# Gathering the next group inside the current one, taps behind the first projection weights, and the 64-row way back first

## Chip, core and metric

The kernel runs on one core of a Trainium2 chip. The core has five engines that matter here: PE (TensorE, matrix products), DVE (VectorE), ACT (ScalarE), POOL (GpSimd) and SP (SyncE, which here only issues DMAs). Data comes from HBM by 16 DMA engines. The metric is the time of one execution on the device, in microseconds.

## What is computed

Two layers over 256 tokens of width 1024, all in float32. The even layer mixes by a gated DeltaNet and a 2-D DFT, the odd layer by a Conformer convolution; both end in the same mixture of experts. Cut to what matters:

```
for l in range(2):
    h = rmsnorm(x) * (1 + sc1) + sh1
    mix = hybrid_mixer(h, ...) if l == 0 else conformer_conv(h, w1, b1, dw_w, ..., w2, b2)
    x = x + g1 * mix
    x = x + g2 * moe_ffn(rmsnorm(x) * (1 + sc2) + sh2, ...)

def conformer_conv(h, w1, ...):            # w1 is 1024 x 2048, dw_w has 31 taps per channel
    val, gate = split(h @ w1 + b1)
    u = depthwise_conv(val * sigmoid(gate), dw_w) + dw_b
    return silu(layernorm(u)) @ w2 + b2

def moe_ffn(t, ...):                       # 32 experts in 8 groups of 4; a token takes 2 experts of one group
    for e in range(32):
        hid = silu(t @ w_gate[e]) * (t @ w_up[e])       # 1024 -> 512
        y = y + combine[:, e] * (hid @ w_down[e])       # 512 -> 1024
```

The weights of the 64 experts are 384 MB, nearly all that is read.

## The kernel before

**The weight ring.** All large weights pass through one ring of 17 slots of 1 MB (tiles `rb`, `rx`, `ra`, `rc`). The list `plan` holds the units in the order of their transfers; an expert is six units (gate and up in two halves each, then down in two). `Ring.pump` (L232) issues the next unit as soon as a slot is free, all on SP's queue, and `Ring.done` frees slots after their last reader. A unit of kind "z" takes a slot without a transfer, as room for a result.

**A layer's experts.** `moe(l)` goes through the 8 groups. How many tokens chose group g is known only on the chip, so for each group the code holds five programs (`ARMS`): for up to 32 tokens, 64, 64 and 32 side by side, 128, and 128 twice. `arms` picks one by compare-and-branch on every engine; each program ends with a jump out over the others. In the profiled execution group 4 of layer 0 and groups 4 and 5 of layer 1 run the 64+32 program, groups 0 and 6 of layer 0 the 64-row one, and the other eleven the 32-row one.

**The gather.** `place` (L1276) brings a group's tokens together: DVE makes a one-hot `oh`, sixteen products with it fill two PSUM banks `px` (L1286), ACT and DVE copy these to `xg`, and a few small products give the combine weights and the transposed one-hot `oc`. `prep(g + 1)` stands behind group g's program, before the jump into the next one. `xg` and `oc` are double, by the parity of the group.

**A group's program** (`group`). For each of its four experts: gate and up products in two halves (`gate_up`, L1345 for 32 rows and L1347 for 64), `hidden` (SiLU on ACT, then a product with the combine weight on DVE), and between the halves of the next expert the down products of the last one (`down`): transposes `pth`, a copy `hT` on DVE, the products `yacc` (L1375 for 32 rows, L1385 for 64). A 64+32 group has two parts, which share the weights. At the end `close` copies `yacc` to `ysb`, and `scatter` is the way back: for each of eight blocks `pso` of the output, one product for each part (L1431) and one DVE operation that adds it to the stream `xT` (L1432).

**Into the odd layer.** In the last group of layer 0 the way back also writes the convolution's input `z`. The projection w1 (`conf_w`) is four blocks of two units; the first two blocks (four units) serve the first half of the channels. The convolution goes by transforms of the taps: `taps_transform`, which needs the taps (two transfers of 31 rows of 4 KB) and the table `dft` (1 MB), stands in PE's program right behind the first tile of the projection (L1540), before the second tile.

Of the kernel before, what the change touches and what calls it, by code (L numbers as in the profile page):

```python
# [310 lines left out]
def build(nc, tc, A, ctx, dbg=None):  # L311
# [39 lines left out]
    ident = C("ident")  # L351
# [138 lines left out]
    with ExitStack() as c0:  # L490
# [29 lines left out]
        add("x", [lambda t: [(t[32 * q:32 * q + 31, 0:1024], A["taps"]) for q in range(2)], A["dft"]])  # L520
        add("w", blk(A["conf_w1"], 0) + blk(A["conf_w1"], 2))
        add("z", [None] * 2)
        add("w", blk(A["conf_w1"], 1) + blk(A["conf_w1"], 3))
# [648 lines left out]
    def moe(l):  # L1172
        with ExitStack() as c1:
# [126 lines left out]
            class Part:  # L1300
# [61 lines left out]
                def down(self, us, hid, j):  # L1362
                    n, first, last = self.n, j == 0, j == 3
                    pt = pg.tile([P, 512], F32, name="pth", tag="tr")
                    hT = m2.tile([P, 4, 128], F32, name="hT", tag="hT")
                    if n == 32:
                        for i in range(2):
                            te.transpose(pt[:, 64 * i:64 * i + 64], hid[:, 128 * i:128 * i + 128], ident[0:64, 0:64])  # L1368
                        hT = hT[:, 0]
                        ve.tensor_copy(hT, pt[:, 0:128])  # L1370
# [6 lines left out]
                    for k in range(4):  # L1377
                        te.transpose(pt[:, n * k:n * k + n], hid[:, 128 * k:128 * k + 128], ident[0:n, 0:n])
                    ve.tensor_copy(hT[:, :, 0:n], pt[:, 0:4 * n].rearrange("p (k s) -> p k s", k=4))
# [37 lines left out]
            def scatter(parts, sums):  # L1417
# [4 lines left out]
                if sums and l == 0:  # L1422
                    zid, zt = ring.take(2, "z")
                    for h, t in enumerate(zt):
                        ve.tensor_copy(t[:, 0:1028].rearrange("p (k c) -> p k c", c=257)[:, :, 256:257], MOD(1, 0)[:, 4 * h:4 * h + 4].unsqueeze(2))
                    zs.append((zid, [t[:, 257 * i:257 * i + 257] for t in zt for i in range(4)]))
                for i, k in enumerate(KORD):
                    o = ps[k // 2][:, 256 * (k % 2):256 * (k % 2) + 256]
                    for p_ in parts:
                        a, b = p_.back(k)  # L1430
                        te.matmul(o, a, b, start=p_ is parts[0], stop=p_ is parts[-1])  # L1431
# [15 lines left out]
            def group(g, arm):  # L1447
# [11 lines left out]
                def tail(j, ids, us, hids):  # L1459
                    for p_, hid in zip(parts, hids):  # L1460
                        p_.down(us, hid, j)
                    ring.done(ids[4:])

                late = None
                for j in range(4):
# [5 lines left out]
                    if late:  # L1471
                        tail(*late)
                    for p_ in parts:
# [29 lines left out]
            for g in range(8):  # L1503
# [4 lines left out]
                if g < 7:  # L1508
                    prep(g + 1)
# [274 lines left out]
```

## Time and profile before

| | |
|---|---|
| median of 3 runs | 1555.91 us (1552.68 to 1557.39) |
| profiled execution | 1556.92 us, of it 1555.0 us span |
| PE busy | 1260.5 us (81%) |
| DVE, ACT, POOL busy | 478.0, 239.6, 152.5 us |
| DMA | 489.68 MB, mean 315 GB/s over the span |

The span is the time from the first to the last instruction in the trace, and all times of the trace are counted from its start. The experts of layer 0 take about 360 to 860 us, the convolution up to 1020 us, the experts of layer 1 the rest. Busy shares are means over stages with different limits; the rows further down are by stage.

### The profile page before, as it was taken

Reading aid. Unit: us, or ns where it says so; the run is one execution under the profiler, and the core shown is the slowest. Engines: PE = TensorE matmul, PEld = TensorE weight load, DVE = VectorE, ACT = ScalarE, POOL = GpSimd, SP = SyncE. Lnnn points to the kernel's source line nnn. Section 1 sums busy time; section 2 is a strip of 40 time slices with the busy share of each in tenths; the row PEclk is TensorE's granted clock in tenths of the full one; section 3 lists DMA queues with packets and bytes.
Section 4 is the critical chain, followed back from the end, with each engine's and each line's share of the span. In section 5 each row is a group of like instructions: output and inputs, shape, how many; then the busy total and the mean of one; then the engine's idle time right before and its main releaser. Section 6 shows DMA issues by size and latency. Waiting matters only on the chain.

```text
span 1555.0 us, 25396 instructions
## 1 busy us (share of the span) xinstructions
PE 1260.5 (81%) x10776; PEld 731.9 (47%) x10776; DVE 478.0 (31%) x1340; ACT 239.6 (15%) x530; POOL 152.5 (10%) x124
## 2 busy tenths in 40 slices
PE   6886999987986666998777499797667679899974
PEld 2443666665554333345444377664344233433542
DVE  3479898773111101012011312321101011201112
ACT  3333333213000000001001201320000000000101
POOL 0556553100000000000000100100000000000000
PEclk8889899987987777999899699998777789899876
DMA  9556665458999999997999942249999999579695
GB/s 351 188 197 215 210 218 187 149 203 336 416 410 415 414 415 413 408 364 299 413 415 406 332 176 108 109 181 414 415 414 414 415 413 409 233 298 352 251 412 207
DMA packets 109446, 489.68 MB, mean 315 GB/s; under 512 B 9474, under 2 KB 19970, under 8 KB 75968
## 3 DMA queue, kind: packets, MB, share of 16 engines
q1 hardware_dynamic: 109248, 487.08, 80.1%
q8 instruction: 120, 1.97, 0.5%
q14 instruction: 78, 0.64, 0.1%
HBM read 486.00 MB, written 1.05 MB: 313 GB/s over the span
## 4 chain that ended last, share of the span: by engine, by line
PE 55%; DMA 29%; DVE 9%; issue 3%; POOL 2%; ACT 2%; SPq 0%; DVEq 0%; ACTq 0%; POOLq 0%
PE gu L1347 10%; PE gu L1345 8%; DMA rb<-down 5%; PE yacc L1385 5%; DMA ra<-up 4%; DMA rc<-up 4%; PE yacc L1375 3%; PE pu L1666 3%; DMA rb<-gate 3%; PE pso L1431 3%; DMA rx<-up 2%; PE pu L1706 2%; PE pp L1040 2%; DMA rb<-up 1%; DMA rc<-down 1%
## 5 line engine op out<-in xcount | busy, mean ns | idle before, releaser
L1345 PE MATMUL gu<-rb,xg 128*32 128x256 f32 x1840 | 159.0, 416 | 33.8 <-DMA rb<-gate 9.9
L1358 DVE SCALAR_TENSOR_TENSOR hid<-sg,dup,gu 64x256 f32<-64x256 f32 (+1 forms) x76 | 42.0, 552 | 444.0 <-ACT sg L1357 357.0
L1357 ACT ACTIVATE sg<-gu 64x256 f32<-64x256 f32 (+1 forms) x76 | 32.9, 433 | 563.1 <-PE gu L1345 343.4
L1347 PE MATMUL gu<-rb,xg 128*64 128x512 f32 x368 | 110.0, 630 | 11.8 <-DMA rc<-gate 4.8
L1345 PEld LDWEIGHTS gu<-rb,xg 128*32 128x32 f32 x1840 | 72.3, 117 | 94.7 <-issue 43.1
L604 POOL TENSOR_TENSOR rc<-rc,sbc 128x1024 f32<-128x1024 f32 x36 | 89.6, 2494 | 42.4 <-DMA rc<-ada_t 42.2
L1345 PE MATMUL gu<-rx,xg 128*32 128x256 f32 x624 | 75.0, 420 | 13.5 <-DMA rx<-gate 4.6
L1040 PE MATMUL pp<-h,ra 128*128 128x512 f32 (+1 forms) x192 | 79.8, 557 | 4.9 <-DVE vtm L1026 4.9
L1431 PE MATMUL pso<-dup,ysb 32*128 32x256 f32 (+1 forms) x304 | 69.5, 463 | 14.2 <-ACT ysb L1401 6.3
L1345 PE MATMUL gu<-ra,xg 128*32 128x256 f32 x656 | 66.8, 430 | 17.0 <-DMA ra<-gate 9.2
L1432 DVE SCALAR_TENSOR_TENSOR xT<-pso,mods,xT 128x256 f32<-128x256 f32 x128 | 53.4, 478 | 64.8 <-PE pso L1431 64.7
L607 DVE SCALAR_TENSOR_TENSOR rc<-rc,sbc 128x1024 f32<-128x1024 f32 x44 | 65.5, 1492 | 4.0 <-DMA rc<-ada_t 3.9
L1345 PE MATMUL gu<-rc,xg 128*32 128x256 f32 x464 | 54.8, 449 | 13.0 <-DMA rc<-gate 8.9
L1375 PE MATMUL yacc<-rb,hT 128*32 128x256 f32 x976 | 61.9, 387 | 2.7 <-DVE hT L1370 2.7
L1347 PEld LDWEIGHTS gu<-rb,xg 128*64 128x64 f32 x368 | 35.4, 143 | 56.9 <-issue 50.5
L1431 PEld LDWEIGHTS pso<-dup,ysb 32*128 32x128 f32 (+1 forms) x304 | 34.7, 196 | 47.7 <-issue 14.6
L1370 DVE COPY hT<-pth 128x128 f32<-128x128 f32 x56 | 16.3, 290 | 131.7 <-PE pth L1368 131.7
L1040 PEld LDWEIGHTS pp<-h,ra 128*128 128x128 f32 x192 | 36.9, 201 | 39.3 <-issue 31.7
L415 POOL TENSOR_TENSOR ttok<-ttok 128x256 f32<-128x256 f32 x4 | 3.0, 752 | 528.8 <-ACT ttok L413 528.7
L1442 POOL TENSOR_TENSOR rb<-xT,a 128x256 f32<-128x256 f32 x5 | 3.4, 691 | 499.3 <-DMA rb<-conf_w 498.9
L1345 PEld LDWEIGHTS gu<-rx,xg 128*32 128x32 f32 x624 | 31.9, 118 | 36.1 <-issue 14.4
L1345 PEld LDWEIGHTS gu<-ra,xg 128*32 128x32 f32 x656 | 28.9, 120 | 41.1 <-issue 13.4
(719 smaller groups left out, 1955.6 us busy)
## 6 DMA issues: line engine op xcount, KB each, us to landing
rb<-down SPq DMA_DIRECT2D x70, 1024.0 KB, 20.1
rb<-gate SPq DMA_DIRECT2D x67, 1024.0 KB, 20.0
rb<-up SPq DMA_DIRECT2D x65, 1024.0 KB, 20.0
rc<-ada_t SPq DMA_DIRECT2D x80, 512.0 KB, 4.4
ra<-gate SPq DMA_DIRECT2D x24, 1024.0 KB, 18.3
ra<-up SPq DMA_DIRECT2D x24, 1024.0 KB, 17.0
rx<-down SPq DMA_DIRECT2D x24, 1024.0 KB, 15.4
rx<-up SPq DMA_DIRECT2D x23, 1024.0 KB, 20.0
```

The source lines that it names most:

```text
L604: ge.tensor_tensor(w, w, sbc, op=ALU.mult)
L607: ve.scalar_tensor_tensor(w, w, 1.0, sbc, op0=ALU.mult, op1=ALU.mult, accum_out=mods[:, l, j:j + 1])
L1040: te.matmul(pp[:, 0:n], w[:, k, o:o + 128], h[:, k, 512 - n:512], start=k == 0, stop=k == KT - 1)
L1345: te.matmul(self.out[o:o + 32], x, w[:, 256 * fh:256 * fh + 256], **how)
L1347: te.matmul(self.out[hf], x, w, **how)
L1357: se.activation(sg, g, AF.Silu)
L1358: ve.scalar_tensor_tensor(hid, sg, self.cw[:, j:j + 1], u, op0=ALU.mult, op1=ALU.mult)
L1375: te.matmul(self.y[32 * q:32 * q + 32], hT[:, o:o + 32], w[:, 256 * q:256 * q + 256], start=first and k == 0, stop=last and k == 3)
L1385: te.matmul(y[hf], hT[:, k, 0:n], w[:, 512 * hf:512 * hf + 512], start=(alone or first) and k == 0, stop=(alone or last) and k == 3)
L1431: te.matmul(o, a, b, start=p_ is parts[0], stop=p_ is parts[-1])
L1432: ve.scalar_tensor_tensor(xT[:, k, :], o, g2[:, k:k + 1], xT[:, k, :], op0=ALU.mult, op1=ALU.add)
L1666: te.matmul(pvg[hf], (wv, wg)[hf](k, 128 * i, 128 * i + 128), h1[:, k], start=k == 0, stop=k == KT - 1)
```

## The change

Three things. The gather of the next group moves from behind the group's program into it: into the third expert, between the down products of the second and the second half of the gate and up products. In the plan, the taps and dft move behind the first four projection units and the two z units. In a group with several parts, all parts are now transposed first (`turn`) before the down products, and on the way back all eight products of the first part come before those of the last.

```
@@ plan
-        add("x", [lambda t: [(t[32 * q:32 * q + 31, 0:1024], A["taps"]) for q in range(2)], A["dft"]])
         add("w", blk(A["conf_w1"], 0) + blk(A["conf_w1"], 2))
         add("z", [None] * 2)
+        add("x", [lambda t: [(t[32 * q:32 * q + 31, 0:1024], A["taps"]) for q in range(2)], A["dft"]])
         add("w", blk(A["conf_w1"], 1) + blk(A["conf_w1"], 3))
@@ Part
-                def down(self, us, hid, j):
+                def turn(self, hid):
...
+                    return hT
+
+                def down(self, us, hT, j):
...
@@ scatter
+                O = lambda k: ps[k // 2][:, 256 * (k % 2):256 * (k % 2) + 256]
+
+                for p_ in parts[:-1]:
+                    for k in KORD:
+                        te.matmul(O(k), *p_.back(k), start=p_ is parts[0] and k % 2 == 0, stop=False, skip_group_check=True)
                 for i, k in enumerate(KORD):
-                    o = ps[k // 2][:, 256 * (k % 2):256 * (k % 2) + 256]
-                    for p_ in parts:
-                        a, b = p_.back(k)
-                        te.matmul(o, a, b, start=p_ is parts[0], stop=p_ is parts[-1])
+                    o = O(k)
+                    te.matmul(o, *parts[-1].back(k), start=len(parts) == 1, stop=True, skip_group_check=len(parts) > 1)
@@ group
                 def tail(j, ids, us, hids):
-                    for p_, hid in zip(parts, hids):
-                        p_.down(us, hid, j)
+                    turned = [p_.turn(hid) for p_, hid in zip(parts, hids)]
+                    for p_, hT in zip(parts, turned):
+                        p_.down(us, hT, j)
...
                     if late:
                         tail(*late)
+                    if j == 2 and g < 7:
+                        prep(g + 1)
                     for p_ in parts:
                         p_.gate_up(us, 1)
@@ moe
                 arms(g, regs[g], 0, len(ARMS))
-                if g < 7:
-                    prep(g + 1)
```

How instructions move on two engines, first at the one place of SP's queue. This is SP's program in the 32-row program of layer 0's last group, before (`down` are the last expert's units, numbers are the slots):

```order
L250 DMA ra_127<-down 128x2x1024
L250 DMA ra_126<-down 128x2x1024
L246 DMA rx_2661<-taps 31x1024 x2
L250 DMA rb_3023<-dft 128x2048
L250 DMA rb_3024<-conf_w 128x4x512
L250 DMA rb_3025<-conf_w 128x4x512
L250 DMA rb_3026<-conf_w 128x4x512
L250 DMA rb_3027<-conf_w 128x4x512
L250 DMA rb_3030<-conf_w 128x4x512
```

and in the changed kernel:

```order
L250 DMA ra_127<-down 128x2x1024
L250 DMA ra_126<-down 128x2x1024
L250 DMA rx_2661<-conf_w 128x4x512
L250 DMA rb_3023<-conf_w 128x4x512
L250 DMA rb_3024<-conf_w 128x4x512
L250 DMA rb_3025<-conf_w 128x4x512
L246 DMA rb_3028<-taps 31x1024 x2
L250 DMA rb_3029<-dft 128x2048
L250 DMA rb_3030<-conf_w 128x4x512
```

Four units of the projection are now ahead of the taps and dft, and nothing else is in another place. On PE, the end of a group's 64+32 program and what follows it until the next group's program, before (`rc_99`, `rx_2662` are the last expert's down slots; the rows of `px` and `po` stand behind the jump):

```order
L1378 MATMUL pth<-cm,hid 128x64 x4
L1385 MATMUL yacc<-rc_99,hT 64x512 x4
L1385 MATMUL yacc<-rx_2662,hT 64x512 x4
L1368 MATMUL pth<-cm,hid 128x64 x2
L1431 MATMUL pso<-dup,ysb 128x256
L1375 MATMUL yacc<-rc_99,hT 32x256 x8
L1375 MATMUL yacc<-rx_2662,hT 32x256 x8
L1431 MATMUL pso<-dup,ysb 128x256 x15
L1496 UNCONDITIONAL_BRANCH
```

and in the changed kernel, where L1438 is the first part's way back and L1441 the last part's:

```order
L1373 MATMUL pth<-cm,hid 128x64 x4
L1392 MATMUL yacc<-rc_99,hT 64x512
L1369 MATMUL pth<-cm,hid 128x64 x2
L1392 MATMUL yacc<-rc_99,hT 64x512 x3
L1392 MATMUL yacc<-rx_2662,hT 64x512 x4
L1385 MATMUL yacc<-rc_99,hT 32x256 x8
L1385 MATMUL yacc<-rx_2662,hT 32x256 x8
L1438 MATMUL pso<-dup,ysb 128x256 x8
L1441 MATMUL pso<-dup,ysb 128x256 x8
L1509 UNCONDITIONAL_BRANCH
```

The 32-row transposes stand inside the 64-row down products, and the sixteen products of the way back are in two blocks instead of alternating. Third, the rows behind that jump on PE, before:

```order
L1286 MATMUL px__9484<-oh,ttok 128x128 x8
L1286 MATMUL px__9497<-oh,ttok 128x128 x8
L1295 MATMUL po__9510<-comb,oh 128x4 x2
L1297 MATMUL po__9510<-cm,oh 128x128 x2
L1487 TENSOR_LOAD cnt
L1496 COMPARE_AND_BRANCH x2
```

In the changed kernel only the load of the count and the two compares are left there, and the gather is in the third expert of the 64+32 program, between the transposes and the second half of its gate products:

```order
L1373 MATMUL pth<-cm,hid 128x64 x4
L1369 MATMUL pth<-cm,hid 128x64 x2
L1286 MATMUL px__10881<-oh,ttok 128x128 x3
L1392 MATMUL yacc<-ra_126,hT 64x512 x4
L1392 MATMUL yacc<-rx_2661,hT 64x512 x4
L1385 MATMUL yacc<-ra_126,hT 32x256 x8
L1385 MATMUL yacc<-rx_2661,hT 32x256 x8
L1286 MATMUL px__10881<-oh,ttok 128x128 x5
L1286 MATMUL px__10894<-oh,ttok 128x128 x8
L1295 MATMUL po__10907<-comb,oh 128x4 x2
L1297 MATMUL po__10907<-cm,oh 128x128 x2
L1347 MATMUL gu<-rb_3025,xg_3160 64x512
```

The gather stands at this place in each of the five programs.

## Rows read from the trace of the kernel before

**Rows 1.** By stage: length, five engines' busy time, PE clock, DMA share, GB/s.

```profile
690.00:711.00 21.00, 20.23 (x134) 12.44 (x134) 5.44 (x14) 2.63 (x7) 0.00 (x0) 0.76 0.33 123
711.00:858.00 147.00, 117.44 (x1067) 64.87 (x1056) 23.54 (x60) 13.69 (x32) 1.19 (x2) 0.91 1.02 411
858.00:864.00 6.00, 0.87 (x3) 0.15 (x1) 3.51 (x11) 2.56 (x8) 3.67 (x6) 0.50 0.45 136
864.00:900.00 36.00, 22.13 (x93) 16.98 (x94) 9.49 (x28) 6.09 (x12) 0.00 (x0) 0.70 1.02 376
900.00:1038.00 138.00, 125.97 (x673) 99.28 (x675) 41.07 (x118) 28.61 (x59) 7.47 (x9) 0.95 0.31 111
...
1340.00:1365.00 25.00, 21.72 (x112) 12.43 (x112) 5.31 (x14) 2.44 (x7) 0.00 (x0) 0.80 0.21 82
...
1430.00:1455.00 25.00, 24.11 (x178) 15.01 (x173) 5.85 (x15) 3.00 (x8) 0.00 (x0) 0.73 0.38 135
1455.00:1530.00 75.00, 55.43 (x672) 30.43 (x668) 10.16 (x28) 4.89 (x13) 0.00 (x0) 0.80 1.01 411
```

**Rows 2.** Timeline of PE: start, length, line, operation, wait before it.

```profile
876.96 1.20 PE L1540 MATMUL pu<-rb,rb 128*128 128x257 f32 x2 [18.09 <-DMA rb<-conf_w]
...
887.78 1.99 PE L1567 MATMUL ptap<-rx,rb 31*128 31x512 f32 x8
```

**Rows 3.** Timeline of SP's queue at the end of layer 0's experts.

```profile
830.23 2.85 SPq L250 DMA_DIRECT2D ra<-down  x2
835.26 4.41 SPq L246 DMA_DIRECT2D rx<-taps  x2
840.32 4.79 SPq L250 DMA_DIRECT2D rb<-dft  x1
```

**Rows 4.** DMA issues from 820 to 900 us: count, size, us to landing.

```profile
ra<-down SPq DMA_DIRECT2D x2, 1024.0 KB, 20.3
...
rb<-dft SPq DMA_DIRECT2D x1, 1024.0 KB, 25.5
```

**Rows 5.** Timeline of POOL, the last writing of z.

```profile
860.56 1.36 POOL L1442 TENSOR_TENSOR rb<-xT,a 128x256 f32<-128x256 f32 x2
```

**Rows 6.** Timeline of PE, 64+32 group of layer 0 and next group's start.

```profile
685.11 1.89 PE L1385 MATMUL yacc<-rx,hT 128*64 128x512 f32 x8
...
688.09 1.07 PE L1375 MATMUL yacc<-rc,hT 128*32 128x256 f32 x16
...
689.96 10.35 PE L1431 MATMUL pso<-dup,ysb 64*128 64x256 f32 x30
701.08 3.61 PE L1286 MATMUL px__11059<-oh,ttok 128*128 128x128 f32 x16 [0.77 <-DVE oh L1280]
704.52 1.95 PE L1286 MATMUL px__11072<-oh,ttok 128*128 128x128 f32 x16
...
707.02 0.41 PE L1345 MATMUL gu<-rx,xg 128*32 128x256 f32 x2
```

**Rows 7.** Timeline of PE, the two 64+32 groups of layer 1.

```profile
1338.41 10.28 PE L1431 MATMUL pso<-dup,ysb 64*128 64x256 f32 x30
...
1358.00 3.65 PE L1347 MATMUL gu<-rb,xg 128*64 128x512 f32 x16 [2.39 <-issue]
...
1430.87 10.57 PE L1431 MATMUL pso<-dup,ysb 64*128 64x256 f32 x30
...
1449.64 0.41 PE L1345 MATMUL gu<-rb,xg 128*32 128x256 f32 x2
```

**Rows 8.** Timeline of all engines, ends of a 32-row and a 64-row group.

```profile
734.54 3.23 DVE L1432 SCALAR_TENSOR_TENSOR xT<-pso,mods,xT 128x256 f32<-128x256 f32 x8 [3.29 <-PE pso L1431]
...
742.34 3.47 PE L1286 MATMUL px__12634<-oh,ttok 128*128 128x128 f32 x16 [5.40 <-issue]
...
804.73 3.15 PE L1431 MATMUL pso<-dup,ysb 64*128 64x256 f32 x16 [0.50 <-ACT ysb L1403]
...
805.19 0.30 PEld L1431 LDWEIGHTS pso<-dup,ysb 64*128 64x128 f32 x4 [0.16 <-DVE ysb L1404]
```

More of the change, by code (lines that the diff above doesn't have):

```diff
@@ L1360, in hidden @@
                     return hid
-                def down(self, us, hid, j):
-                    n, first, last = self.n, j == 0, j == 3
+                def turn(self, hid):
+                    n = self.n
                     pt = pg.tile([P, 512], F32, name="pth", tag="tr")
@@ L1368, in down @@
                             te.transpose(pt[:, 64 * i:64 * i + 64], hid[:, 128 * i:128 * i + 128], ident[0:64, 0:64])
+                        ve.tensor_copy(hT[:, 0], pt[:, 0:128])
+                    else:
+                        for k in range(4):
+                            te.transpose(pt[:, n * k:n * k + n], hid[:, 128 * k:128 * k + 128], ident[0:n, 0:n])
+                        ve.tensor_copy(hT[:, :, 0:n], pt[:, 0:4 * n].rearrange("p (k s) -> p k s", k=4))
+                    return hT
+                def down(self, us, hT, j):
+                    n, first, last = self.n, j == 0, j == 3
+                    if n == 32:
                         hT = hT[:, 0]
-                        ve.tensor_copy(hT, pt[:, 0:128])
                         for k in range(4):
@@ L1376, in down @@
                         return
-                    for k in range(4):
-                        te.transpose(pt[:, n * k:n * k + n], hid[:, 128 * k:128 * k + 128], ident[0:n, 0:n])
-                    ve.tensor_copy(hT[:, :, 0:n], pt[:, 0:4 * n].rearrange("p (k s) -> p k s", k=4))
                     alone = self.y is None
```

## The prediction

> **What bounds the kernel now.** I read the table by stage first, for the share of time in which the DMA engines are busy [rows 1]. From 711 to 858 us and from 1455 to 1530 us it is 1.01 to 1.02 at 411 GB/s: there the expert weights stream without a gap, and PE waits for them. A transfer cannot come sooner there unless the queue started sooner. So what counts is where the queue stands still, and there are four such places [rows 1]: 690 to 711 us (share 0.33, 14 us idle), 858 to 864 and then 900 to 1038 us (0.45 and 0.31, the way into the odd layer and its convolution, with PE busy 125.97 of 138 us), 1340 to 1365 us (0.21, 20 us idle) and 1430 to 1455 us (0.38, 15 us idle). In these PE sets the pace: the 17 ring slots are full, and the next transfer waits until PE has read a slot. A microsecond taken from PE inside such a place, or just ahead of it, is a microsecond off the end, since all behind it is a stream at a fixed rate; a microsecond taken from PE elsewhere is only more waiting.
>
> I then read the PE rows of these places. The idle stretches at 690, 1340 and 1430 us are the way back of the three groups that run the 64+32 program, with the jump and the gather behind it [rows 6, 7]. The one at 858 us is a wait of PE: 18.09 us until a block of conf_w has landed [rows 2].
>
> **Term A, the order of the taps.** Before, SP issues the last expert weights (the second ends at 833.08), the taps at 835.26, dft until 845.11, and then the first projection weights [rows 3]. The expert weights land 20.3 us after issue, dft 25.5 [rows 4]: at 853.4 and 870.6. Between these lie 17.2 us for 1.3 MB, which at the 376 GB/s of the stage behind [rows 1] should take 3.4. The queue is not fast there: from 858 to 864 it moves 136 GB/s [rows 1]. The taps, two transfers of 31 rows, are what differs from all others. PE starts its first product at 876.96 and comes to the taps' product at 887.78, 10.8 us later [rows 2].
>
> Now four weight units go first. At 376 GB/s 1.05 MB takes 2.8 us, so the third, with which PE can start, lands at 853.4 + 8.4 = 861.8 and the fourth at 864.6. The other operand, z, is written until 861.92 by the last POOL row [rows 5]. PE starts at about 862.3, 14.7 us sooner, and is done with this first tile at 873.1. But the next thing in PE's program is the taps' product, and that is not moved. If taps and dft behind the weights still take 17.2 us, they are there at 864.6 + 17.2 = 881.8. PE stands still again, 8.7 us, and goes on at 881.8 instead of 887.78: **A = 6.0 us**. The bounds: 14.7 if taps and dft are there when PE comes to them (at 873.1), and 0 if they need 23 us. I stay with 17.2, the only measured length. What queues behind dft, the second block of the projection, is needed four tiles of the convolution later.
>
> The Trainium skill, DMA: Bandwidth & Descriptors, "Why a DMA increments its semaphore by 16 and not by 1", says that a transfer is spread over the largest number of engines up to 16 that divides its rows. With 31 rows that is one engine, and at the about 27 GiB/s that the page gives it the two transfers of 124 KB would keep it 8.8 us (an estimate from the page), with 2.8 for dft 11.6 in all and A = 11.6 by it. The 17.2 us of this trace agree with the kind of delay, not with its size; I take the trace.
>
> **Term B, the three groups of 64+32 rows.** These are group 4 of layer 0 and groups 4 and 5 of layer 1. What changes in one:
> The gather (sixteen products, the counts, the transposes) moves into the third expert. Warm, its second eight products and the small ones take 707.02 - 704.52 = 2.5 us and the first eight then 1.8: **+4.3 us**, in a stretch where PE has nothing to wait for. The cold first eight cost 3.61 in the old place [rows 6].
> With both turns first, the 32-row turn hides in the 64-row down products. Before, 2.96 us pass from their end (687.00) to the long way back (689.96), and the 32-row down products, from 688.09 on, are 1.87 of it [rows 6]: **-1.1**.
> The way back: before, 64-row and 32-row products alternate for 10.35, 10.28 and 10.57 us [rows 6, 7]. No row shows eight 64-row products without VectorE behind them. Bounds: 3.15 with it, and in that group the first pair gives way to the second after 0.46 us, so four pairs are 1.9 [rows 8]; I take 1.9, for nothing reads them yet. The 32-row eight are then paced by eight VectorE operations of 3.23 us together [rows 8]. 1.9 + 3.2 = 5.1: **-5.2**.
> The boundary: last way-back product to the first product of the next group is 6.7 us (700.31 to 707.02), 9.3 (1348.69 to 1358.00) and 8.2 (1441.44 to 1449.64) [rows 6, 7]. The gather is gone from it, but the jumps stay. Jumping out of a program costs 5.40 us where nothing else is queued, as behind the 32-row program at 742.34 [rows 8]; at 701.08 it is hidden, since only 0.77 is idle there, and PE waits for VectorE [rows 6]. The new way back ends on VectorE like the 32-row one, so little can be queued. The jump into the 64+32 program costs 2.39 [rows 7]. I take 4.5 for the way out (between 2.39 and 5.40), 2.4 more where the next group is again 64+32, and 1.7 for the clock: after such a gap the first eight gather products took 3.61 and the next eight 1.95 [rows 6], and now the gate products stand there. That is 6.2, 8.6 and 6.2: **-0.5, -0.7, -2.0**.
> Sum: 3 x (4.3 - 1.1 - 5.2) - 3.2 = -9.2. The bounds: with 5.40 for each of the four jumps 9.2 - 5.7 = 3.5 us are left, with 2.39 for each way out it is 15.5. **B = 9 us**, less than the 49 us of idle DMA that it can be taken from.
>
> **At nothing.** In the other eleven groups the gather moves too, and so does a gap of some 5 us behind it. PE waits there for landings, and the share of 1.01 to 1.02 says that the queue never ran dry [rows 1]; the cover is that wait, which is gone only if PE fell behind by the slots already filled. Turning a single part is what it was. The ring serves the same number of units in the same order but for the six.
>
> **Sum.** 6.0 + 9 = 15 us from the profiled execution of 1556.92 us (span 1555.0 and 1.92 around it) is 1541.9. The median of the three runs, 1555.91, is 1.0 lower, which makes **1541 us**; with the end that I trust least, the jumps, in mind I put it at 1543.
>
> **The rivals.**
> (Times on the median's scale.) No change: the two gains go into waits that take their place. Taps and dft need 23 us or more behind the weights, so that PE waits for them until 887.78 as now, and jumps of 5.40 leave 3.5 of B: 1552.4 us. For it: PE's order is fixed, so the wait moves rather than goes. Against: the 17.2 us are measured with other transfers already among them.
> More: the taps are there at 873.1 (A = 14.7), and the jumps cost 2.39 (B = 15.5): 1555.9 - 30.2 = 1525.7; one of the two alone gives 1532.2 or 1534.4. For it: at 701.08 a jump out is hidden [rows 6]. Against: there PE had slow alternating products queued.
> Slower: two taken jumps now stand back to back. In the old order the gather's products lay between them, and PE could run these while the second program was fetched. If a jump with nothing queued takes d more than I took it for, four of them lie on the path: B is gone at d = 2.3, A too at 3.8, and a slowdown of 0.3% begins at d = 5.0, which is some 9.5 us for a way out. At d = 6 the time is 1555.9 - 15.2 + 24 = 1565. The Trainium skill, Runtime: NRT & Kernel Launch, "Instruction fetch mechanics", speaks against this change here: a taken branch breaks the sequential prefetch, and a target outside the window is fetched before execution goes on. The trace agrees that a jump shows, with 5.40 us at 742.34 [rows 8], but has none as long as 9.
> The gather that does not move in effect: if its products waited in the third expert for VectorE's one-hot, the 4.3 us would be more; VectorE is busy for 5.31 of the 25 us around such a boundary [rows 1], so I give it little.
>
> **How the numbers follow.** 0.3% of this kernel, 4.7 us, is about what its runs can tell from no change. My case (1536 to 1550) has 0.60, no change (1550 to 1558) 0.15, more than forecast (1524 to 1536) 0.17, slower (above 1558) 0.08. From 1532 to 1553 I leave out about 2 in 10. Faster by over 0.3% (below 1551.2) takes my case, the upper one and a little of no change: 0.78; within 0.3%: 0.14; slower: 0.08.
>
> **What would show it.** A is right if PE's first projection product starts near 862, and the taps' product is preceded by a wait for DMA of 6 to 10 us and starts near 880; that wait gone means A was too small, a start past 887 that it was nothing (both less what B saved before). B is right if the way back of a 64+32 group lasts 5 us instead of 10.3, the gather in the third expert 4.3, and PE's gap between groups is issue time of 4 to 7 us; the DMA share at the three places rises by 2 to 5 us each. I am wrong if such a gap is 9 us or more, if the first projection weights are held up in SP's queue, or if a group in the streamed stretches shows DMA shares below 1.

## The result, and the profile after

The change makes the kernel 1% faster: 1540.55 us (median of 4 runs, 1538.68 to 1542.04) against 1556.65 us (4 runs), a ratio of 0.9898 with an interval of 0.9871 to 0.9925, so some 16 us. Forecast were 1543 us, 13 less than the median shown there. The profiled execution took 1542.04 us, with a span of 1540.0.

To see where the time came from, I cut the span at four PE rows: the first gate product of layer 0, the end of its last way-back product, the first gate product of layer 1, and the end of its last way-back product. These are at 380.11, 858.87, 1033.60 and 1540.80 us before, and at 383.67, 861.00, 1026.80 and 1524.81 after:

| stage | before | after | difference |
|---|---|---|---|
| ahead of layer 0's experts | 380.1 | 383.7 | +3.6 |
| experts of layer 0 | 478.8 | 477.3 | -1.4 |
| way into the convolution, convolution | 174.7 | 165.8 | -8.9 |
| experts of layer 1 | 507.2 | 498.0 | -9.2 |
| end | 14.2 | 15.2 | +0.9 |

The first line is no part of the change. In the thirteen profiles of this study that point lies anywhere from 375.7 to 387.0 us, whatever the kernel. So runs differ by some us before the first expert starts, and the stage lengths say more about a cause than two whole times.

A product shows as two records in all rows of PE here (a transpose as one), so x16 are eight products. The stage table of the changed kernel (columns as in [rows 1]; the stretches of layer 1 are set 6 to 10 us earlier, as far as the stream is ahead by then):

```profile
690.00:711.00 21.00, 15.93 (x124) 7.42 (x126) 4.43 (x12) 1.05 (x3) 0.00 (x0) 0.84 0.62 236
711.00:858.00 147.00, 119.42 (x1080) 60.12 (x1072) 21.26 (x53) 12.38 (x29) 0.00 (x0) 0.86 1.02 411
...
1333.60:1358.60 25.00, 15.58 (x102) 6.26 (x104) 3.87 (x11) 1.34 (x3) 0.00 (x0) 0.80 0.35 132
1420.00:1445.00 25.00, 19.59 (x222) 10.22 (x222) 4.91 (x13) 1.50 (x4) 0.00 (x0) 0.86 0.62 236
1445.00:1515.00 70.00, 51.24 (x632) 27.31 (x628) 9.23 (x24) 4.90 (x13) 0.00 (x0) 0.85 1.01 414
```

At the three places behind the 64+32 groups the DMA share rose from 0.33, 0.21 and 0.38 to 0.62, 0.35 and 0.62, which is 6.1, 3.5 and 6.0 us of streaming that used to be idle. The full stretches are as full as before. That is the form in which such a kernel gains: the stream does not run faster, the queue stands still for less time.

PE at the way into the convolution (start, length, then what was idle before and who ended it):

```profile
858.61 2.39 PE L1441 MATMUL pso<-dup,ysb 32*128 32x256 f32 x8 [0.56 <-DVE xT L1442]
866.25 1.20 PE L1551 MATMUL pu<-rb,rb 128*128 128x257 f32 x2 [5.25 <-issue]
...
875.20 2.91 PE L1551 MATMUL pu<-rb,rb 128*128 128x257 f32 x6 [4.33 <-DMA rb<-taps]
...
882.98 1.99 PE L1578 MATMUL ptap<-rb,rb 31*128 31x512 f32 x8
...
886.88 3.72 PE L1677 MATMUL pu<-h,rb 128*128 128x256 f32 x16
```

The wait of 18.09 us [rows 2] is gone. Two idle times stand in its place: 5.25 us of the jump out of the program (the jump's own record on PE runs from 859.79 to 866.08), then 4.33 us for the taps in the middle of a tile that does not read them. The taps' product starts at 882.98 instead of 887.78.

PE at the end of layer 0's 64+32 group, against [rows 6]:

```profile
689.53 1.07 PE L1392 MATMUL yacc<-rc,hT 128*64 128x512 f32 x2 [0.52 <-DVE hT L1374]
690.54 0.33 PE L1369 MATMUL pth<-cm,hid 64*128 64x64 f32 x2
...
694.38 1.07 PE L1385 MATMUL yacc<-rc,hT 128*32 128x256 f32 x16
...
696.24 2.00 PE L1438 MATMUL pso<-dup,ysb 64*128 64x256 f32 x16
...
699.44 1.87 PE L1441 MATMUL pso<-dup,ysb 32*128 32x256 f32 x8 [0.56 <-DVE xT L1442]
705.82 0.64 PE L1345 MATMUL gu<-rx,xg 128*32 128x256 f32 x2 [4.51 <-issue]
```

The way back lasts 5.07 us (696.24 to 701.31) instead of some 10, and behind it PE is idle for 4.51 us, where it was for 0.77. The other two groups read the same, with 8.86 us (a jump out and a jump into a 64+32 program) and 4.85. (The load of the count and two compares lie in these gaps too; from the end of the jump's record to that of the last compare it is 0.7 us where no compare jumps.)

### The profile page after: what moved, and what is told of

Its sections match the earlier page's. It is cut to its first block, busy times and chain, and to the rows that moved or that the text cites. A ratio compares the mean times of both kernels' runs of the same rounds, so it can differ in the third digit from the quotient of the medians.

```text
span 1540.0 us, 25408 instructions
## 1 busy us (share of the span) xinstructions
PE 1238.1 (80%) x10776; PEld 699.3 (45%) x10776; DVE 477.6 (31%) x1340; ACT 239.5 (16%) x530; POOL 152.9 (10%) x124
## 4 chain that ended last, share of the span: by engine, by line
PE 51%; DMA 32%; DVE 9%; issue 3%; POOL 3%; ACT 1%; SPq 0%; DVEq 0%; POOLq 0%; ACTq 0%
PE gu L1347 10%; PE gu L1345 9%; DMA rb<-down 7%; PE yacc L1392 5%; DMA rb<-up 5%; DMA rc<-down 4%; DMA rx<-up 4%; PE pu L1677 3%; PE yacc L1385 3%; DMA ra<-gate 3%; DMA ra<-up 3%; PE pu L1717 2%; POOL rc L604 1%; DMA rb<-taps 1%; DVE rc L607 1%
## 5 line engine op out<-in xcount | busy, mean ns | idle before, releaser
L1345 PE MATMUL gu<-rb,xg 128*32 128x256 f32 x1824 | 164.8, 423 | 53.4 <-issue 19.0
L1345 PE MATMUL gu<-ra,xg 128*32 128x256 f32 x656 | 76.2, 474 | 28.7 <-issue 10.4
L1345 PE MATMUL gu<-rx,xg 128*32 128x256 f32 x640 | 81.1, 443 | 19.4 <-issue 10.8
L1345 PE MATMUL gu<-rc,xg 128*32 128x256 f32 x464 | 58.1, 482 | 15.8 <-issue 7.5
L1345 PEld LDWEIGHTS gu<-ra,xg 128*32 128x32 f32 x656 | 32.3, 131 | 57.1 <-issue 33.3
L1441 PE MATMUL pso<-dup,ysb 32*128 32x256 f32 (+1 forms) x256 | 43.3, 443 | 14.7 <-DVE xT L1442 7.8
L1347 PE MATMUL gu<-rx,xg 128*64 128x512 f32 x128 | 46.5, 625 | 6.4 <-issue 6.4
L1326 ACT COPY dup<-pdup 128x260 f32<-128x260 f32 x19 | 7.1, 376 | 263.0 <-PE pdup L1325 263.0
## 6 DMA issues: line engine op xcount, KB each, us to landing
ra<-up SPq DMA_DIRECT2D x24, 1024.0 KB, 17.8
rx<-down SPq DMA_DIRECT2D x24, 1024.0 KB, 15.5
```

The costliest lines, as they stand in the source:

```text
L1345: te.matmul(self.out[o:o + 32], x, w[:, 256 * fh:256 * fh + 256], **how)
L1347: te.matmul(self.out[hf], x, w, **how)
L1441: te.matmul(o, *parts[-1].back(k), start=len(parts) == 1, stop=True, skip_group_check=len(parts) > 1)
```

## The experiments

Eleven kernels, each with 5 to 10 runs beside the kernel before. The stage columns are the difference to before in the profiled execution, cut at the same PE rows as above. Stages of kernels that don't differ there mostly agree within some 3 us (experts 1 of e1_taps, -2.7, is such a stage); the convolutions of e9 and e10 differ by 4.7. "Faster" and "slower" in us below are from the ratios; between two kernels of this table they are uncertain by 4 to 6 us.

| kernel | median us | ratio to before, interval | experts 0 | convolution | experts 1 |
|---|---|---|---|---|---|
| changed kernel | 1540.55 | 0.9898 (0.9871 to 0.9925) | -1.4 | -8.9 | -9.2 |
| e1_taps: order of the taps alone | 1548.98 | 0.9957 (0.9939 to 0.9976) | +1.4 | -1.1 | -2.7 |
| e2_gather: gather alone | 1546.65 | 0.9946 (0.9927 to 0.9965) | -0.4 | -1.3 | -9.8 |
| e3_back: turn and way back alone | 1548.82 | 0.9951 (0.9929 to 0.9973) | -2.8 | 0.0 | -6.6 |
| e8_oldback: changed, old way back | 1545.35 | 0.9943 (0.9922 to 0.9964) | +0.8 | -7.4 | -5.5 |
| e4_taps16: changed, taps split | 1532.53 | 0.9845 (0.9824 to 0.9866) | -2.7 | -11.1 | -8.8 |
| e7_twoarms: changed, one wait less | 1535.67 | 0.9887 (0.9864 to 0.9909) | -0.7 | -11.8 | -9.9 |
| e5_end: changed, gather at the end | 1543.28 | 0.9920 (0.9902 to 0.9938) | +1.5 | -7.5 | -3.8 |
| e6_end16: e4 and e5 | 1539.06 | 0.9894 (0.9875 to 0.9913) | -0.9 | -12.0 | -4.7 |
| e11_ahead: changed, products ahead | 1530.42 | 0.9832 (0.9808 to 0.9856) | -6.1 | -7.5 | -15.1 |
| e9_ahead16: e4 and e11 | 1524.62 | 0.9804 (0.9776 to 0.9832) | -5.7 | -13.9 | -15.1 |
| e10_first16: e9, first gather outside | 1523.84 | 0.9802 (0.9774 to 0.9829) | -11.9 | -9.2 | -12.3 |

### Each part alone

**The order of the taps alone.** The kernel before, with the one moved line of the plan.

> The kernel before with the new order of the plan alone (taps and dft behind four projection units). By the prediction -6.0 us against before. By the trace of the changed kernel -7.3: there the stream was 1.0 us late when the experts of layer 0 ended and 6.3 us early behind the convolution. PE then waits about 4 us for the second taps transfer inside the first projection tile, and the taps' product starts some 5 to 8 us sooner than 887.8. Rival: the gain in the changed kernel came from the groups ahead of it, and the order of the taps alone gives less than 2 us.

By its ratio it is 6.7 us faster (interval 3.7 to 9.5). That speaks for the forecast and against the rival. Its profiled execution, 1553.28 us, is at the upper end of its runs (1544.47 to 1554.73) and shows how the gain can shrink:

```profile
876.03 2.91 PE L1540 MATMUL pu<-rb,rb 128*128 128x257 f32 x6 [6.46 <-DMA rb<-taps]
...
884.85 1.99 PE L1567 MATMUL ptap<-rb,rb 31*128 31x512 f32 x8
...
889.33 6.47 PE L1666 MATMUL pu<-h,rb 128*128 128x256 f32 x16
```

The wait for the taps is 2.1 us longer than in the changed kernel, and the sixteen records behind the taps take 6.47 us where they take 3.72 there. The granted clock was 0.72 over that stretch (884 to 896 us) and 1.00 over the changed kernel's (884 to 891). So the stage is only 1.1 us shorter here.

**The gather alone.**

```
@@ group
+                    if j == 2 and g < 7:
+                        prep(g + 1)
@@ moe
-                if g < 7:
-                    prep(g + 1)
```

> The kernel before with the gather moved into the third expert alone; way back and turn as before. By the prediction's terms: +4.3 us for the gather in each of the three 64+32 groups and -0.5, -0.7 and -2.0 at the boundaries, so about 10 us slower. Rival: behind the slow alternating way back the jump out is hidden, as it was before the change (0.77 us idle), so the boundaries shrink from 6.7, 9.3 and 8.2 us to about 1, 3 and 1, which is -20 in all against at most +13: 5 to 15 us faster.

8.4 us faster, so the rival holds and not the sum by my terms. The row of layer 0's 64+32 group (the first gate product stands behind the jump):

```profile
689.07 9.94 PE L1431 MATMUL pso<-dup,ysb 64*128 64x256 f32 x30
699.74 0.64 PE L1345 MATMUL gu<-rx,xg 128*32 128x256 f32 x2 [0.73 <-DVE xT L1432]
...
1346.36 4.15 PE L1347 MATMUL gu<-rb,xg 128*64 128x512 f32 x12 [6.26 <-issue]
```

Behind the slow way back the jump out costs nothing to be seen: 0.73 us are idle. The boundary was 6.7 us and is 0.7. It is not so at all three: between layer 1's two 64+32 groups (the last row), where a jump in follows the jump out, 6.26 us stay idle, and behind the second of them 1.76.

**Turn and way back alone.** The kernel before, with the new `turn`, `down` and `scatter` of the change.

> The kernel before with turn and way back of the 64+32 groups alone; the gather stays behind the program. The way back gives -5.2 us in each of three groups. If the jump out, no longer hidden, takes 4.5 us there and the gather behind it stays at 5.5 to 6, each boundary grows by 3.5 to 4: -4 to -5 us in all. Rival: the jump stays hidden, and -15 us come whole.

7.6 us faster, between the two numbers and nearer to the first theory. The boundary shows that theory's mechanism (layer 0's 64+32 group, then the old gather):

```profile
699.68 1.87 PE L1441 MATMUL pso<-dup,ysb 32*128 32x256 f32 x8 [0.56 <-DVE xT L1442]
705.09 3.78 PE L1286 MATMUL px__11059<-oh,ttok 128*128 128x128 f32 x16 [3.54 <-issue]
...
712.19 0.41 PE L1345 MATMUL gu<-rx,xg 128*32 128x256 f32 x2
```

The jump that was hidden (0.77 us idle, [rows 6]) now shows with 3.54, with no load of a count in it, and the gather behind it takes longer than before. From the last way-back product to the next gate product it is 10.6 us instead of 6.7.

The three parts alone sum to -22.7 us, and together they give some -16. The times don't show where the rest is lost. By the next run the way back gives 7.0 us on top of the other two, about the 7.6 that it gives alone, while these two, 15.1 us if added, give 8.9 together; each of these numbers is uncertain by some us. What the way back loses to the jump, it loses alone as well as with the others.

**The changed kernel with the old way back.** `scatter` as before, all else of the change.

> The changed kernel with the old alternating way back. By the prediction's terms the new one is worth 3 times 5.2 us, so about 1556. Rival, from the runs with one part alone (taps -6.7, gather -8.4, way back -7.6, all three -16.0): way back and gather gain the same microseconds, since the slow alternating products hide the jump: within 2 us of the changed kernel, about 1541.

8.9 us faster than before, some 7 less than the changed kernel (the two intervals overlap only from 0.9922 to 0.9925). So it lies between the rival and my terms. Its rows say why the new way back gives so much less than it is shorter:

```profile
692.96 12.20 PE L1438 MATMUL pso<-dup,ysb 64*128 64x256 f32 x32
705.89 0.64 PE L1345 MATMUL gu<-rx,xg 128*32 128x256 f32 x2 [0.73 <-PE pso L1438]
```

From the first way-back product to the next gate product it is 12.9 us here and 9.6 in the changed kernel, so 3.4 less, though the way back is 7.1 us shorter. For the groups of layer 1 the same rows give 14.2 against 13.9 (0.3) and 13.8 against 9.9 (3.8): 7.5 us are left of 22.6. The jump takes back the rest, since the slow way back covers it (0.73, 1.62 and 0.73 us idle in this run) and the fast one does not (4.51, 8.86, 4.85).

### The way into the convolution

**The taps over more DMA engines.**

```
-        add("x", [lambda t: [(t[32 * q:32 * q + 31, 0:1024], A["taps"]) for q in range(2)], A["dft"]])
+        add("x", [lambda t: [(t[32 * q + o:32 * q + o + n, 0:1024], A["taps"][o:o + n]) for q in range(2) for o, n in ((0, 16), (16, 15))], A["dft"]])
```

> The changed kernel with each transfer of the taps split into one of 16 and one of 15 rows. If it is the 31 rows on a single DMA engine that make taps and all behind them late (62 rows of 4 KB in 12.8 us), then the four transfers land together with their neighbours, the wait of 4.33 us inside the first tile and the late sixteenth part of dft (7.8 us) are gone, and the taps' product starts near 877 instead of 883: 5 to 6 us faster than the changed kernel, about 1535. Rival: the rows are slow wherever they go, or two more transfers cost as much: within 1.5 us of the changed kernel.

1532.53 us, 24.1 faster than before by its ratio and 8.2 faster than the changed kernel by the two ratios. PE's rows:

```profile
862.06 1.20 PE L1551 MATMUL pu<-rb,rb 128*128 128x257 f32 x2 [6.63 <-DVE xT L1718]
...
873.09 1.99 PE L1578 MATMUL ptap<-rb,rb 31*128 31x512 f32 x8
```

and the DMA issues from 845 to 880 us (count, size, us from issue to landing), first dft in the changed kernel, then this run:

```profile
rb<-dft SPq DMA_DIRECT2D x1, 1024.0 KB, 22.8
...
rb<-dft SPq DMA_DIRECT2D x1, 1024.0 KB, 12.9
rb<-taps SPq DMA_DIRECT2D x2, 64.0 KB, 12.6
rb<-taps SPq DMA_DIRECT2D x2, 60.0 KB, 11.3
```

The first tile runs through in 11.0 us (16.7 in the changed kernel), and dft lands 12.9 us after issue; in the changed kernel it took 22.8, before 25.5 [rows 4]. The bytes are the same and there are two transfers more. So 31 rows in one transfer were what made taps and all behind them late. The price is less sure than the cause: 8.2 us by the time, but the stage is only 2.2 us shorter than in the changed kernel, and the taps' product comes 4.3 us sooner behind the last way back. The other two pairs with and without the split (e6 against e5, e9 against e11) differ by 4.0 and 4.4 us, so 4 to 8 us are shown. The Trainium skill, DMA: Bandwidth & Descriptors, "Why a DMA increments its semaphore by 16 and not by 1", says that the engines of a transfer are the largest number up to 16 that divides its rows; 31 rows give one, 16 and 15 rows give 16 and 15. The traces agree with it: in the changed kernel the semaphore of each taps transfer takes one step when it lands (868.64 and 875.06 us), and here 16 for a transfer of 16 rows and 15 for one of 15.

**The wait on a semaphore of another program.** The PE program of the changed kernel, with the semaphores that a product waits for, at the first tile:

```
L1551 MATMUL pu_16880<-rb_3026,rx_2661 128x257 [waits DMAHW7_49,DMAHW5_49]
L1551 MATMUL pu_16881<-rb_3027,rb_3025 128x257 [waits DMAHW4_49,DMAHW2_49]
```

In the 32-row program the projection unit `rb_3025` is issued on DMAHW2 and the second taps transfer on DMAHW4. In the 64+32 program and the two larger ones the taps go ahead of that unit, and it is issued on DMAHW4. The product stands behind all five programs and waits for both. So in the 32-row program it waits for the taps, which it does not read. In this run layer 0's last group has only the two smaller programs:

```
-                arms(g, regs[g], 0, len(ARMS))
+                arms(g, regs[g], 0, 2 if (l, g) == (0, 7) else len(ARMS))
```

> The changed kernel without the three larger programs in layer 0's last group, which takes the 32-row program in this data (for other data the output would be wrong). That changes nothing that runs but one wait: PE's third projection product no longer waits on the semaphore that belongs to the second taps transfer in the 32-row program and to a projection unit in the larger ones. Taps stay on one DMA engine and land at 875.1, dft at 877.3. Theory: the first tile runs through to about 877, the taps' product starts near 877.5 instead of 883, about 5 us faster than the changed kernel, 1535. Rival: the late DMA engine alone sets it, and it is within 1.5 us of the changed kernel.

```profile
860.65 1.20 PE L1551 MATMUL pu<-rb,rb 128*128 128x257 f32 x2 [5.26 <-issue]
...
872.06 1.99 PE L1578 MATMUL ptap<-rb,rb 31*128 31x512 f32 x8 [0.53 <-DMA rb<-dft]
```

The wait is gone, and the tile takes 11.4 us, 5.3 less, as the theory has it; the taps' product now waits 0.53 us for dft. The stage is 2.9 us shorter than in the changed kernel, no more than such stages scatter. The time, 0.9887 against 0.9898 (1.7 us), does not tell 5 us from none. So the mechanism is shown and its price is not.

### What hides a jump

**The gather at the program's end.**

```
@@ group
-                    if j == 2 and g < 7:
-                        prep(g + 1)
...
                 scatter(parts, g == 7)
+                if g < 7:
+                    prep(g + 1)
```

> The changed kernel (1540.5 us) with the gather at the end of each program, behind the way back and ahead of the jump, instead of in the third expert. Theory: PE runs what is queued while it jumps, as it did behind the slow way back (0.73 us idle there when the gather alone was moved, 4.5 when nothing was queued). The sixteen products, some 3.8 us, then cover most of the jump; the boundaries stay near 4.5, 8.9 and 4.9 us and the gather's cost inside the three groups (about 0, 2 and 4 us) is gone: some 6 us faster, 1534 to 1536. Rival: only slow queued work hides a jump, the products and the jump add up, and the boundaries grow by 3.8 to 5.6 each: 5 to 11 us slower, 1546 to 1551.

> Both together: gather at the program's end and taps in transfers of 16 and 15 rows. The two lie at different places, so what the first gives or costs comes on top of the 8.0 us of the second: 1526 to 1528 if the jump is covered, 1538 to 1543 if not.

1543.28 and 1539.06 us: by the ratios 3.4 slower than the changed kernel (not clear of the noise by itself), and 7.6 slower than the one with split taps. The rival wins, with a smaller loss than it named. Layer 0's 64+32 group:

```profile
700.25 2.05 PE L1286 MATMUL px__11087<-oh,ttok 128*128 128x128 f32 x16
...
704.29 0.42 PE L1297 MATMUL po__11113<-cm,oh 128*128 128x128 f32 x2
708.48 0.41 PE L1345 MATMUL gu<-rx,xg 128*32 128x256 f32 x2 [3.77 <-issue]
```

Some 4.5 us of products ahead of the jump made the idle time only 0.74 us shorter (4.51 to 3.77); at the two boundaries of layer 1 it is 2.4 and 2.6 us (8.86 to 6.49, 4.85 to 2.25). Queued work as such does not hide the jump. In the new way back the last products wait for VectorE, whose operations pace them, and the gather's products have waits of their own. In the old way back PE is the slower of the two, and a product waits for an operation on its bank that is four pairs back.

When a jump begins and ends can be read from its record on PE (count, then shortest, median and longest in ns, then first and last start in us). Layer 0's 64+32 group in the kernel before, in the changed kernel and in e5:

```profile
L1496 PEldq COMPARE_BRANCH  x1: 5497/5497/5497, 693.1 to 693.1; - x1
L1509 PEldq COMPARE_BRANCH  x1: 4267/4267/4267, 700.6 to 700.6; - x1
L1509 PEldq COMPARE_BRANCH  x1: 4833/4833/4833, 702.6 to 702.6; - x1
```

Before, the jump starts 7.2 us ahead of the end of the way back (693.13, 700.31) and is over while PE still works off products. In the changed kernel it starts 0.70 us ahead of that end, in e5 2.28 us behind it, in the gather. In the first two it starts at the fourth of the eight VectorE operations, for which the last product waits: the operation ends at 693.07 and 700.56, the jump starts at 693.13 and 700.61 (e2 and e8: 1335.10 and 1335.16, 697.31 and 697.37). So a jump runs beside queued products from the moment at which the last wait is passed.

**Products ahead.** The theory was that a jump starts once PE's program has passed its last wait. So I took the waits from the end of the way back, by issuing the last part's eight products before the eight VectorE operations:

```
@@ scatter
-                for i, k in enumerate(KORD):
-                    o = O(k)
-                    te.matmul(o, *parts[-1].back(k), start=len(parts) == 1, stop=True, skip_group_check=len(parts) > 1)
+                for k in KORD:
+                    te.matmul(O(k), *parts[-1].back(k), start=len(parts) == 1, stop=True, skip_group_check=len(parts) > 1)
+                for i, k in enumerate(KORD):
+                    o = O(k)
                     ve.scalar_tensor_tensor(xT[:, k, :], o, g2[:, k:k + 1], xT[:, k, :], op0=ALU.mult, op1=ALU.add)
```

> The changed kernel (1540.5 us) with only that: all products of the last part of the way back ahead of the VectorE operations, taps as they were. The three boundaries give 4.5 to 6 us, the way into the convolution nothing, since there PE waits for the taps behind it: 1534.5 to 1536. Rival: no gain, 1539 to 1542.

> The kernel with split taps (1532.5 us) and, on the way back, all products of the last part ahead of the eight VectorE operations instead of one by one with them. Theory: a jump starts when PE's program has passed its last wait. Now the last four products wait for VectorE, so the jump begins with the last of them; with no such wait the last product comes 1.3 to 1.7 us sooner and the jump runs while VectorE still adds. Each of the three 64+32 boundaries gets 1.5 to 2 us shorter, and so does the way into the convolution: 4 to 8 us faster, 1525 to 1528. Rival: the next program's first product needs what VectorE still holds, and the wait moves there: within 1.5 us of 1532.5.

1530.42 and 1524.62 us. By the ratios e11 is 10.3 us faster than the changed kernel, more than expected, and e9 6.4 faster than e4. The same boundary of layer 1 behind a 32-row group, in the changed kernel:

```profile
1114.00 1.87 PE L1441 MATMUL pso<-dup,ysb 32*128 32x256 f32 x8 [0.56 <-DVE xT L1442]
1122.18 0.64 PE L1345 MATMUL gu<-rx,xg 128*32 128x256 f32 x2 [6.31 <-issue]
```

and with the products ahead:

```profile
1104.95 1.15 PE L1440 MATMUL pso<-dup,ysb 32*128 32x256 f32 x16 [0.52 <-ACT ysb L1408]
1112.23 0.64 PE L1345 MATMUL gu<-rx,xg 128*32 128x256 f32 x2 [6.14 <-issue]
```

The eight products take 1.15 us instead of 3.1 (1112.72 to 1115.87), and from the first of them to the next gate product it is 7.3 us instead of 9.5. The jump, in the changed kernel and here:

```profile
L1509 PEldq COMPARE_BRANCH  x1: 6059/6059/6059, 1115.2 to 1115.2; - x1
L1510 PEldq COMPARE_BRANCH  x1: 6206/6206/6206, 1105.0 to 1105.0; - x1
```

It takes as long as before but starts 0.07 us behind the first of the eight products instead of 2.45, as the theory has it. The two boundaries between a 32-row group and a 64+32 one became 2 us shorter in the same way. But behind the 64+32 groups the first way-back product and the next gate product came closer by only 0.5, 0.2 and 1.2 us:

```profile
689.75 2.00 PE L1438 MATMUL pso<-dup,ysb 64*128 64x256 f32 x16
691.67 1.15 PE L1440 MATMUL pso<-dup,ysb 32*128 32x256 f32 x16
698.82 0.64 PE L1345 MATMUL gu<-rx,xg 128*32 128x256 f32 x2 [6.00 <-DMA rx<-down]
```

```profile
L1510 PEldq COMPARE_BRANCH  x1: 6140/6140/6140, 691.7 to 691.7; - x1
```

The row names a transfer, but the gate product comes 0.98 us behind the end of the jump (697.84), as it does in the changed kernel (0.94). The jump starts 2.4 us sooner here and lasts 6.14 us instead of 4.27, and so in layer 1 (6.17 for 4.21, 5.88 for 4.62); why it lasts longer stays open. So the 10 us are not the three boundaries that I counted, and the number expected of e9 came in for another reason. By the rows the three give 1.9 us, the two ways into a 64+32 group behind a 32-row one 4.5, and each layer's last way back some 2.

**The first gather outside.** e9 with `prep(1)` of layer 0 behind the first group's program.

> The kernel with split taps and the products ahead, and the gather for layer 0's second group back behind the first group's program. In the kernels with the gather in the third expert, the stream of weights fell 1 to 2 us behind during that first group (64 rows, ring just filled), and did not in those without. If that loss comes from the gather's 4.3 us, it is gone here: 1 to 2 us faster than the kernel with split taps and products ahead, which the trace shows more surely than the time. Rival: the loss is not the gather's, and the stream falls behind there as before.

1523.84 us, the same as e9 within the interval. In the profile the experts of layer 0 are 6.2 us shorter than in e9 and the convolution behind them is 4.7 longer, so that gain was not kept in this execution; why is not shown.

## Why the prediction was right

**The sum** was right: 15 us worked out, put at 13, and 16 measured (by stages -8.9 where A had -6.0, and -10.6, which is -1.4 and -9.2, where B had -9.2; the scatter of a stage is some 3 us). That PE sets the pace at the idle places, and that the taps hold up the queue, held. But inside A and inside B errors of both signs cancelled, so that the total came so near is partly luck.

**Term A.** That SP's queue behind the expert weights is slow because of the taps held: e4 takes the slowness away with the same bytes. The 17.2 us were misread. The 25.5 us of dft count from the start of its issue at 840.32 [rows 3, 4], so it landed at 865.8 and not 870.6, and 12.5 us lie between it and the expert weights. With these the sum would have had dft at 877.1 behind the moved weights, and A at 10.7; in the changed kernel it landed at 877.3. The other estimate in the prediction, 11.6 us, was nearer than the 17.2 that it went by. Against that, two things were left out. The projection units landed at 862.46 and 865.85, near the forecast 861.8 and 864.6, but PE started at 866.25 and not 862.3: the jump out of the last program, which the wait of 18 us had covered. And a wait of 4.33 us came inside the tile, on the taps' semaphore (the second transfer landed at 875.06), instead of 8.7 at the taps' product, which then waited for nothing. It started at 882.98 where I had 881.8: near by luck. With the stream 2.1 us later at that point (861.00 against 858.87), the 4.8 us become 6.9, against 6.0. The remaining 2 us of the stage come behind it, where the next 32 records take 7.2 us (886.88 to 894.05) and took 8.86 before.

**Term B.** Its terms against the rows, all three 64+32 groups together:

| | forecast | measured |
|---|---|---|
| gather inside the program | +12.9 | +12.7 |
| turn, way back | -3.3, -15.6 | -15.7 |
| boundaries behind the groups, with the clock | -3.2 | -0.6 |
| ways into group 4 of each layer | 0 | -8.8 |
| start of layer 0's first group | 0 | +2.1 |
| sum | -9.2 | -10.3 |

The gather was right. From the first to the last gate and up product, where PE has no idle time, the groups take 67.0, 67.0 and 65.3 us before and 71.8, 71.3 and 71.0 in the changed kernel, of which 1.9 in the third is the clock. The second of them (length, busy time of the engines, clock, DMA share, GB/s), before and after:

```profile
1263.85:1330.89 67.04, 67.04 (x551) 26.15 (x552) 6.31 (x13) 4.24 (x9) 0.00 (x0) 0.97 1.00 404
```

```profile
1252.73:1324.02 71.29, 71.29 (x589) 29.98 (x590) 7.68 (x17) 6.13 (x14) 0.00 (x0) 0.97 1.01 409
```

The way back was sized right: 5.07 us against 5.1. The turn's -1.1 did not come: the 32-row transposes stand inside the 64-row down products, and these now take 4.85 us (689.53 to 694.38) where they took 3.7 (683.34 to 687.00), so the wait went to the front. From the last gate and up product to the last way-back product it is 12.7 us in each group instead of 17.8 to 18.1. At the boundaries PE is idle for 4.51, 8.86 and 4.85 us, and then the gate products run at half clock, as put down for the first of them. The first 32 records of them, before and after:

```profile
707.02:708.96 1.94, 1.94 (x34) 1.01 (x33) 0.86 (x3) 0.38 (x1) 0.00 (x0) 1.00 0.00 0
```

```profile
705.82:709.46 3.64, 3.64 (x33) 1.62 (x33) 0.00 (x0) 0.00 (x0) 0.00 (x0) 0.50 0.00 0
```

A granted clock of 0.50 is the level of 1.2 GHz, and 1.7 us are lost by it, as forecast; PE had stood still for 4.51 us before the fall is seen. With it the first boundary is 6.2 us, the forecast number. The second is 8.86 and 1.9 more (its first sixteen records take 5.53 us, before 3.65), 10.8 where I had 8.6; the third 6.6 for 6.2. So the boundaries gave -0.5, +1.5 and -1.6 for -0.5, -0.7 and -2.0: the price of a jump in behind a jump out was too low.

**At nothing** is the step that failed, though it didn't spoil the sum: "PE waits there for landings". Ahead of group 4 of each layer PE did not wait. The first weights of these groups landed 20.1 and 20.0 us ahead of the first gate product before (595.29 and 1243.90 us), and 15.6 and 15.7 ahead in the changed kernel, since no gather stands at that boundary any more. PE was behind the stream there and set the pace from there on, so the 4.5 and 4.3 us count. (The profile names a transfer before some of these gate products; it is not one that they read.) In the other kernels with the gather in the third expert it is 15.5 to 16.3 us (e2, e4, e7, e8) or, with the products ahead, 13.2 to 13.4 (e9, e10, e11); in those without it there 18.5 to 21.5.

The other thing put at nothing is layer 0's first group, where the stream has just begun. Its first gate products, before and after:

```profile
380.11 5.33 PE L1347 MATMUL gu<-rx,xg 128*64 128x512 f32 x16 [4.78 <-issue]
```

```profile
383.67 4.32 PE L1347 MATMUL gu<-rx,xg 128*64 128x512 f32 x10 [5.13 <-issue]
389.22 1.93 PE L1347 MATMUL gu<-rx,xg 128*64 128x512 f32 x6 [1.23 <-issue]
```

In the changed kernel PE breaks off after ten records, the sixteen take 7.5 us, and the ring's slots come free some 2 us later from there on: from 395 to 415 us the queue moves 386 GB/s at a DMA share of 0.99 instead of 419 at 1.02, which is the sign of being wrong that the prediction named. It is not the work of the gather, which begins only at 410.55. All kernels with the gather in this group's program show the break (0.79 to 1.35 us), e5 and e6 too, where it stands at the program's end; e1, e3 and e10, which have it behind the program, don't. What holds PE up is not shown.

**The rivals.** Slower did not come, though the gaps that it feared are there: behind the 32-row and 64-row programs PE is idle for 6.2 to 6.4 us, and for 13.0 to 13.4 where the next program is one for 64 rows or 64+32. There two jumps follow each other, here ahead of layer 0's group 6 (the shortest, 76 ns, is a compare that does not jump):

```profile
L1509 PEldq COMPARE_BRANCH  x3: 76/5976/6838, 743.4 to 750.0; - x3
```

The queue kept moving over these gaps (402 GB/s from 604 to 618 us), and the gather's products, which lay between the two jumps before, are gone from them. Between the two 64+32 groups the gap of 8.86 us is 9.12 and 9.43 in e7 and e4, at the limit that I had set. Against "more than forecast" I had written that slow alternating products hide the jump; e2 and e8 show that this was the point of the case. The old way back is slow and covers the jump out; the new one is fast and pays for it.

## What to carry to other kernels

When a slow piece of work is made fast, look at what it was hiding: here a jump stood behind it, and two thirds of what became shorter went there. A jump is covered by what is queued when the last wait is passed: products that wait for another engine to the last did not cover it, and putting the products first, and the operations that read them after, gave 10 us. A stage in which PE waits now and then is not one in which PE is ahead: ask at each boundary when the weights landed that its first product reads. And spread small transfers over many rows that divide well: 62 rows in two transfers of 31 made the transfer behind them land some 10 us later, and splitting them gave 4 to 8 us.

## What the runs showed of the hardware that I had not expected

- A product behind a branch over several programs waits for the semaphores of all of them. Where the order of transfers differs between programs, it can wait for a transfer that it does not read (4.33 us in the changed kernel, 6.46 with the order of the taps alone, none with two programs whose order is the same).
- A jump out of a program occupies PE's sequencer for 3.3 to 7.7 us by its record (3.31 at 1435.62 in e5, 7.73 at 435.60 in e9), and a jump in for 3.7 to 7.3; a compare that does not jump takes 0.1. It starts when the last wait ahead of it is passed and runs beside the products that are queued then: 0.73 us of idle PE where 7 us of them were queued (e2, e8), 3.3 to 6.6 behind most ways back of the new kind. Why one jump takes longer than another is not shown.
- The point at which the same first 380 us end differs by up to 11 us between executions (375.7 to 387.0), more than any single part of this change is worth.
